# One decoder layer in fp32: the two gates of the mixer as paired Strassen products

## Chip, core and metric

The kernel runs on one core of a Trainium2 chip. The metric is the device time of one execution in microseconds (us). Three executions of the kernel before took 2221.05, 2221.36 and 2223.29 us; their median is 2221.36. TensorE (PE) multiplies, VectorE (DVE) and ScalarE (ACT) do elementwise work, SyncE (SP) issues the transfers (DMAs). Each engine works through its own instructions in a fixed order and waits on semaphores of the others.

## What is computed

```python
D_MODEL = 2048; SEQ = 256; D_FF = 5504; CONV_WIDTH = 1024
x  = LN0(alpha*x + 0.5*SwiGLU_1(x))
z  = x @ W_in        # columns: conv B | C | h | hgrn q | f | i | g | gate_conv (2048) | gate_hgrn (2048)
yA = B * causal_dwconv3(C * h)                   # 256 x 1024
yB = HGRN2(q, f, i, g)                           # 256 x 1024
m  = sigmoid(gate_conv)*(yA @ Wa) + sigmoid(gate_hgrn)*(yB @ Wb)   # the merge
x  = LN1(alpha*x + m @ W_out)
x  = LN2(alpha*x + 0.5*SwiGLU_2(x))
x  = LN3(alpha*x + sigmoid(x @ W_pg) * (p @ W_pp))
```

Everything is float32. The change touches the line of `m`: the two gate products (256 x 2048 by 2048 x 2048 each) and the turning of `m` for the product with `W_out`.

## The kernel before

**Tiles.** The 256 rows are two row tiles t = 0, 1 of 128. The 2048 columns of an operand are 16 k-tiles of 128; products are made in column chunks of 512 (`CC`). A stationary operand (x, ya, yb, m) is kept transposed, 128 x 128 per k-tile, and split into a high and a low part (names ending in h and l), since each fp32 product is done in three reduced-precision passes: wh·xh, wl·xh, wh·xl (L1052 to L1054 before, L1096 to L1098 after). A matmul has 512 columns.

**Weights.** Each element of the plan of weights is 256 rows by 512 columns, 512 KB. SP loads it into a slot `raw`, of which there are four (`NRAW`). ScalarE casts it to `wh` (L985 before, L1029 after), VectorE forms `wl` = raw − wh (L996, L1040); then the raw slot is free for the next load. Six pairs of wh and wl (`NMAIN`) exist; a pair is free when its last matmul is done. `feed()` hands out loads, additions, casts and splits in the order of the plan as slots allow. A scheduler then fixes the order on each engine.

**Units.** A `Unit` is a plain product: for each chunk of columns, blocks of k-tiles are run for both row tiles into two accumulators (PSUM banks; eight exist, handed to roles such as `a` for accumulators and `t` for transposes), and an epilogue works on each. A `Quad` computes two column chunks at once, for both row tiles. The feed-forward stages use it already. Of its 16 k-tiles eight go through Strassen products (Winograd's form): seven products p1 to p7 in place of eight, for which sums of weight elements (`11`, `t1`, `22`, `t3`, `t2`, `21`, `t4` in two steps `.0` and `.1`) are made by VectorE in place (L964 before, L1008 after), and sums of x (s1 to s4) are stationary operands. The other eight k-tiles are plain: elements `a0` to `a3` for the first chunk (into p2 and p4), `u0` to `u3` for the second. The order of its elements is written out in a string. Weights that enter sums have slots of their own (`raw11` two, `raw12`, `raw21`, `raw22` one each: `HIGH`), which exist only in some stages ("regions").

**The merge before.** For each of four chunks c: a Unit x1 · gate_conv of 16 k-tiles with a sigmoid in its epilogue, then a Unit ya · Wa of 8 k-tiles, whose epilogue multiplies; then the same for four chunks of gate_hgrn and yb · Wb, whose epilogue also adds. Finished tiles of m are turned in the background (`defer` puts a step some ticks, that is some elements, later): the six tiles of c < 3 by VectorE in blocks of 32 x 32 (`turn_blocks`, L297), the two of c = 3 by TensorE against an identity (`to_stat`, L274 before, L278 after). Ahead of the merge stands the convolution, whose last steps (`b`, `z`, `gh`/`gl`: the operand ya) run beside the first gate matmuls. The product with W_out follows.

Of the kernel before, what the change touches and what calls it, by code (L numbers as in the profile page):

```python
# [66 lines left out]
class Quad:  # L67
# [18 lines left out]
    ORDER = ("h1 u0 h2 h3 a0 h4 11.0 u1 t1.0 22.0 t3.0 a1 t2.0 21.0 t4.0 "  # L86
             "11.1 u2 t1.1 22.1 t3.1 a2 t2.1 21.1 t4.1").split()
    ORDER8 = ("u3 a3 11.0 u0 t1.0 a0 22.0 t3.0 u1 t2.0 21.0 a1 t4.0 "
              "11.1 u2 t1.1 22.1 t3.1 a2 t2.1 21.1 t4.1").split()

    def __init__(self, stat, w, cols, width, after, short):
        self.stat, self.w, self.cols, self.width, self.after = stat, w, cols, width, after
        self.shorted = not short
        order = self.ORDER if short else self.ORDER8
# [42 lines left out]
def hybrid_layer(ctx: ExitStack, tc: tile.TileContext, x, p, ln_g, ln_b, ffn1_w_in, ffn1_w_out, mix_w_in,  # L137
# [24 lines left out]
    def open_region(kind):  # L162


        if kind.startswith("tail"):
            region.pop("hctx").close()
        region["pool"] = reopen("ctx", kind, "left")
        region["kind"] = kind
        if kind.startswith("lead"):
            region["high"] = reopen("hctx", kind + "h", "right")  # L170
            held.update(dict.fromkeys(HIGH, 0), on=False)
        if kind.startswith("ffn"):
            roles = {"a": 7, "t": 1}
        else:
            roles = {"t": 2, "a": 4, "h": 2}
# [100 lines left out]

    def halves(stat, t, g, src, nb, tag):

        where, bufs = {"m": (region["pool"], 4), "s": (region["pool"], 7)}.get(tag, (op, 8))
# [5 lines left out]
        nc.vector.tensor_tensor(out=lf, in0=src, in1=hf.bitcast(F32), op=ALU.subtract)  # L285
        stat.parts[t, g] = (h, l)

    def to_stat(stat, t, g, src, nb, tag):
        tp = transposed(src, nb)
        halves(stat, t, g, tp[:, : nb * P], nb, tag)  # L290

    def turn_blocks(dst, src, nb):

        cols = src[:, : nb * P].rearrange("p (a b c) -> p a b c", b=4, c=32)
        for q in range(4):
            for b in range(4):
                nc.vector.transpose(dst[32 * b : 32 * b + 32, :nb, 32 * q : 32 * q + 32], cols[32 * q : 32 * q + 32, :, b, :])  # L297

    def to_stat_blocks(stat, t, g, src, nb, tag):
        y = rtile([P, 4, P], F32, tag="hT", name="hT", bufs=2)  # L300
        turn_blocks(y, src, nb)
        halves(stat, t, g, y[:, :nb, :].rearrange("p a b -> p (a b)"), nb, tag)


    plain = {}
# [5 lines left out]
    def plain_tile(t, c):  # L311
# [2 lines left out]
            plain[t, c // 2] = high(("11", "12", "21", "22")[2 * t + c // 2], "yT")  # L314
        return plain[t, c // 2][:, c % 2, :]

    def sums(stat):
        def both(o, a, b, op):
            nc.vector.tensor_tensor(out=o, in0=a, in1=b, op=op)

        def four(x11, x12, x21, x22, s1, s2, s3, s4):
            both(s3, x11, x21, ALU.subtract)
            both(s1, x21, x22, ALU.subtract)
            both(s2, s1, x11, ALU.subtract)
            both(s4, x12, s2, ALU.add)
# [125 lines left out]
    def ffn(name, xs, w_in, w_out, ln_i, nxt):  # L451
# [7 lines left out]
        def in_units(ch, g, ci):  # L459
            c0 = starts[ch]  # L460
            w = starts[ch + 1] - c0
            if ch > 1:
# [33 lines left out]
                def fifth(ps):  # L496
# [8 lines left out]
                units.append(Quad(xs, w_in, (c0, DFF + c0), CC, after, ch < 10))  # L505
                return
            silu = {}

# [286 lines left out]
    conv_units(1)  # L795

    ms = Stat()
    mc = {}

    def gate_units(c, first):  # L800
        sig = {}

        def epi_s(t, acc):
            sig[t] = st.tile([P, CC], F32, tag="silu", name="sig", bufs=2)
            nc.scalar.activation(sig[t], acc, AF.Sigmoid)

        def epi_y(t, acc):
            if first:
                mc[t, c] = rtile([P, CC], tag=f"m{t}{c}", name="m")
                nc.vector.tensor_tensor(out=mc[t, c], in0=sig[t], in1=acc, op=ALU.mult)  # L810
            else:
                m = mc[t, c]
                nc.vector.tensor_tensor(out=sig[t], in0=sig[t], in1=acc, op=ALU.mult)
                nc.vector.tensor_tensor(out=m, in0=m, in1=sig[t], op=ALU.add)
                turn = to_stat_blocks if c < 3 else to_stat
                defer(2, lambda: turn(ms, t, c, m, 4, "g" if c < 2 else "m"))

        base = 7 * CW if first else 7 * CW + D
        units.append(Unit(x1, wm, 0, 16, base + c * CC, CC, epi_s))
        units.append(Unit(ya if first else yb, (branch_w_conv if first else branch_w_hgrn)[0], 0, 8, c * CC, CC, epi_y))  # L820

    units.append(("merge", drain))
    for c in range(4):
# [53 lines left out]
    for u in units:  # L877
# [3 lines left out]
        if isinstance(u, Quad):  # L881
            base = len(plan)
            for el in u.els:
                if "add" in el:
                    adds.append(len(plan))
                    el["behind"] += base
                for key, ks, n in el.get("load", ()):
# [4 lines left out]
                    loads[ring].append((key, kind, u.w, ks[0] * P, len(ks), u.cols[n], u.width))  # L892
# [181 lines left out]
    def run_quad(u, gi):  # L1074
# [5 lines left out]
        for el in u.els:  # L1080
            for i, (bank, t, ks) in enumerate(el["use"]):
                tick()
                first = bank not in ps
                if first:
                    ps[bank] = ptile("a", bank)
# [10 lines left out]
    for u in units:  # L1096
# [2 lines left out]
        elif isinstance(u, Quad):  # L1099
            gi = run_quad(u, gi)  # L1100
        else:
            if u[0] == "merge":
                u[1]()
            if region["kind"] != u[0]:
                open_region(u[0])
            if u[0] != "merge":
                u[1]()
            feed()
    drain()
# [29 lines left out]
```

## Time and profile before

| | |
|---|---|
| runs, median | 2221.36 us |
| profiled execution | 2221.55 us, span 2219.8 us, granted clock 0.996 |
| TensorE busy | 2193.6 us (99%) in 10062 matmuls |
| VectorE busy | 1748.4 us (79%) |
| ScalarE busy | 1142.0 us (51%) |
| DMA | 430 MB, 194 GB/s on average |
| the merge | 1057 us to 1317 us of the span |

A row of the timeline has the start and the length in us, the engine, the line, the operation, what it writes and reads, its shape, and how many alike follow each other (x2); in brackets stands the idle time ahead of it and what ended that. A row of a group has the busy time, the mean length of one in ns, and the idle time ahead. A row of windows has, for a stretch, the busy time of each engine with its number of instructions, the granted clock of TensorE (1.00 is full), the DMA engines' busy share and GB/s. A row on transfers ends with the size of each and the median time from issue to landing in us.

### The profile page before, as it was taken

What the parts mean: (1) busy time and instruction counts of PE and PEld (TensorE: products, weight loads), DVE (VectorE), ACT (ScalarE), POOL (GpSimd) and SP (SyncE); (2) the same over time, 40 slices, a digit from 0 to 9 for tenths busy, and PEclk for the clock granted to TensorE, in tenths of its full rate; (3) what the DMA queues carried; (4) which work ended last, traced back from release to release, by engine and by line L of the source; (5) the groups of instructions that cost most, each with busy time, mean ns of one, the idle gap of its engine ahead of it and who ended that gap; (6) DMA issues with size and microseconds to landing.
All of it is one profiled execution on the core that took longest, in us unless ns stands there. A gap on an engine that the chain in (4) does not pass through costs nothing.

```text
span 2219.8 us, 27083 instructions
## 1 busy us (share of the span) xinstructions
PE 2193.6 (99%) x10062; PEld 1826.8 (82%) x10062; DVE 1748.4 (79%) x2042; ACT 1142.0 (51%) x1357; POOL 10.0 (0%) x32
## 2 busy tenths in 40 slices
PE   9999999999999999999999999999999999999997
PEld 7988888888877888888888888798888888888886
DVE  6799998999885678557555876779999989998668
ACT  5555555555555534434444443645556555555463
POOL 1000000000000000000000000000000000000000
PEclk9999999999999999999999999999999999999999
DMA  7666666666663665554555675566666666665564
GB/s 252 217 191 210 204 205 193 189 200 209 209 199 105 200 197 173 175 167 152 190 190 190 198 228 194 182 200 199 186 199 194 205 213 200 201 209 181 167 224 154
DMA packets 225848, 430.00 MB, mean 194 GB/s; under 512 B 14252, under 2 KB 22964, under 8 KB 225716
## 3 DMA queue, kind: packets, MB, share of 16 engines
q1 hardware_dynamic: 225716, 428.27, 60.9%
q8 instruction: 79, 1.29, 0.2%
q14 instruction: 53, 0.43, 0.1%
HBM read 426.12 MB, written 2.10 MB: 193 GB/s over the span
## 4 chain that ended last, share of the span: by engine, by line
PE 94%; DVE 3%; ACT 1%; DMA 1%; issue 1%; SPq 0%; DVEq 0%; ACTq 0%
PE bank L1052 30%; PE bank L1053 30%; PE bank L1054 30%; PE bank L274 2%; DVE wl L996 1%; PE bank L643 1%; ACT wh L985 1%; DMA raw<-in_ffn_w_out_dram 1%; DMA raw<-in_ffn_w_in_dram 0%; DVE x L444 0%; DVE silu L469 0%; DMA x<-in_x_dram 0%; DVE x L445 0%; ACT y L424 0%; DVE raw L964 0%
## 5 line engine op out<-in xcount | busy, mean ns | idle before, releaser
L985 ACT CAST wh<-raw 128x1024 fp32r<-128x1024 f32 (+2 forms) x944 | 947.8, 1031 | 808.7 <-PE bank L1054 424.2
L996 DVE TENSOR_TENSOR wl<-raw,wh 128x1024 fp32r<-128x1024 f32 (+2 forms) x944 | 1109.7, 1199 | 303.5 <-ACT wh L985 285.3
L1054 PE MATMUL bank<-wh,xl 128*128 128x512 f32 (+1 forms) x1688 | 651.9, 387 | 1.5 <-DVE xl L285 1.5
L1053 PE MATMUL bank<-wl,xh 128*128 128x512 f32 (+1 forms) x1688 | 652.5, 387 | 0.0
L1052 PE MATMUL bank<-wh,xh 128*128 128x512 f32 (+1 forms) x1688 | 644.3, 388 | 1.6 <-ACT xh L284 1.6
L1054 PEld LDWEIGHTS bank<-wh,xl 128*128 128x128 f32 x1688 | 317.8, 188 | 63.2 <-DVE xl L285 2.2
L1052 PEld LDWEIGHTS bank<-wh,xh 128*128 128x128 f32 x1688 | 318.1, 188 | 62.4 <-ACT xh L284 2.3
L1053 PEld LDWEIGHTS bank<-wl,xh 128*128 128x128 f32 x1688 | 318.1, 188 | 60.4 <-DVE wl L996 0.5
L1052 PE MATMUL bank<-wh,gh 128*128 128x512 f32 x896 | 346.7, 392 | 2.8 <-ACT wh L985 1.4
L1053 PE MATMUL bank<-wl,gh 128*128 128x512 f32 x896 | 348.8, 390 | 0.5 <-DVE wl L996 0.3
L1054 PE MATMUL bank<-wh,gl 128*128 128x512 f32 x896 | 348.2, 390 | 0.0
L964 DVE TENSOR_TENSOR raw<-raw,raw 128x1024 f32<-128x1024 f32 (+1 forms) x176 | 206.3, 1172 | 9.2 <-DMA raw<-in_ffn_w_in_dram 8.0
L1052 PEld LDWEIGHTS bank<-wh,gh 128*128 128x128 f32 x896 | 168.1, 188 | 39.5 <-ACT wh L985 4.8
L1053 PEld LDWEIGHTS bank<-wl,gh 128*128 128x128 f32 x896 | 168.3, 188 | 36.4 <-DVE wl L996 2.2
L1054 PEld LDWEIGHTS bank<-wh,gl 128*128 128x128 f32 x896 | 168.2, 188 | 34.8
L1053 PE MATMUL bank<-wl,sh 128*128 128x512 f32 x464 | 181.6, 391 | 0.0
L1054 PE MATMUL bank<-wh,sl 128*128 128x512 f32 x464 | 180.5, 389 | 0.0
L1052 PE MATMUL bank<-wh,sh 128*128 128x512 f32 x464 | 177.1, 389 | 0.0
L1052 PEld LDWEIGHTS bank<-wh,sh 128*128 128x128 f32 x464 | 87.1, 188 | 18.3
L1054 PEld LDWEIGHTS bank<-wh,sl 128*128 128x128 f32 x464 | 87.1, 188 | 17.9
L1053 PEld LDWEIGHTS bank<-wl,sh 128*128 128x128 f32 x464 | 87.1, 188 | 17.8
L284 ACT CAST gh<-bank 128x512 fp32r<-128x512 f32 (+2 forms) x50 | 28.3, 568 | 76.8 <-PE bank L274 75.7
(173 smaller groups left out, 1018.7 us busy)
## 6 DMA issues: line engine op xcount, KB each, us to landing
raw<-in_ffn_w_in_dram SPq DMA_DIRECT2D x288, 512.0 KB, 4.3
raw<-in_mix_w_in_dram SPq DMA_DIRECT2D x176, 512.0 KB, 4.7
raw<-in_ffn_w_out_dram SPq DMA_DIRECT2D x168, 512.0 KB, 4.6
raw<-in_ffn_w_in_dram SPq DMA_DIRECT2D x64, 256.0 KB, 3.0
raw<-in_mix_w_out_dram SPq DMA_DIRECT2D x32, 512.0 KB, 5.1
raw<-in_ple_w_gate_dram SPq DMA_DIRECT2D x32, 512.0 KB, 5.2
raw<-in_ffn_w_in_dram SPq DMA_DIRECT2D x32, 384.0 KB, 3.8
raw<-in_branch_w_conv_dram SPq DMA_DIRECT2D x16, 512.0 KB, 4.5
```

The costliest lines, as they stand in the source:

```text
L274: state["turned"] = nc.tensor.transpose(tp[:, i * P : (i + 1) * P], src[:, i * P : (i + 1) * P], ident).ins
L284: nc.scalar.copy(hf, src)
L643: nc.tensor.matmul(gp[:, (h * 2 + t) * 64 : (h * 2 + t + 1) * 64], kd[:, h, t * P : (t + 1) * P], qd[:, h, t, :], start=True, stop=True)
L964: nc.vector.tensor_tensor(out=out, in0=a, in1=b, op=ALU.add)
L985: nc.scalar.copy(h[:, :n, :w], raw[:, :n, :w])
L996: state["split"] = nc.vector.tensor_tensor(out=l[:, :n, :w], in0=raw[:, :n, :w], in1=h[:, :n, :w].bitcast(F32), op=ALU.subtract).ins
L1052: nc.tensor.matmul(acc, sh, wh[:, a, :n], start=first, stop=False)
L1053: nc.tensor.matmul(acc, sh, wl[:, a, :n], start=False, stop=False)
L1054: nc.tensor.matmul(acc, sl, wh[:, a, :n], start=False, stop=last)
```

## The change

For each c, the chunk of gate_conv and the chunk of gate_hgrn with the same columns become one Quad, with eight k-tiles by Strassen products. Two new orders are added; that of the first quad ("gate0") has all plain elements of the first chunk ahead. Behind each Quad come the Units ya · Wa and yb · Wb of that c. The sums s1 to s4 of x1 are made once, as the merge begins (`gate_sums`): VectorE adds high and low part to get x back, forms the sums, and both engines split them. The plain elements of the second chunk are added into p3 (t = 0) and into p1's bank under the name `r` (t = 1). The merged tiles are kept, and TensorE turns all eight beside the last branch units. The merge gets the regions' high slots and other shares of banks.

```diff
+        "gate": "a0 a1 11.0 11.1 u0 t1.0 a2 22.0 t3.0 u1 t2.0 21.0 a3 t4.0 u2 t1.1 22.1 t3.1 u3 t2.1 21.1 t4.1",
+        "gate0": "a0 a1 a2 a3 11.0 11.1 u0 t1.0 22.0 t3.0 u1 t2.0 21.0 t4.0 u2 t1.1 22.1 t3.1 u3 t2.1 21.1 t4.1",
...
+        second = (("p3", 0), ("r", 1)) if form.startswith("gate") else (("p3", "d"), ("p5", 1))
...
-            made[f"u{i}"] = dict(load=[(None, ks, 1)], use=[("p3", "d", ks), ("p5", 1, ks)])
+            made[f"u{i}"] = dict(load=[(None, ks, 1)], use=[(*to, ks) for to in second])
...
-    def turn_blocks(dst, src, nb):
...
+    def gate_sums():
+        x = []
+        for t in range(NT):
+            for g in range(2):
+                h, l = x1.parts[t, g]
+                x.append(rtile([P, CC], tag=f"m{t}{g}", name="xT"))
+                nc.vector.tensor_tensor(out=x[-1], in0=h.rearrange("p a b -> p (a b)").bitcast(F32),
+                                        in1=l.rearrange("p a b -> p (a b)").bitcast(F32), op=ALU.add)
+        four(*x, x[2], x[0], s3 := rtile([P, CC], tag="m02", name="xT"), x[1])
+        for n, src in (("s1", x[2]), ("s4", x[1]), ("s3", s3), ("s2", x[0])):
+            halves(x1, n, 0, src, 4, "s")
+
+    def gate_units(c):
...
+        def first(ps):
+            made["conv", 0] = work("h")
+            nc.scalar.copy(made["conv", 0], ps["p1"])
+
+        def second(ps):
+            h = made["hgrn", 0] = work("silu")
+            nc.scalar.copy(h, ps["p3"])
+            both(h, h, ps["p5"], ALU.add)
...
+        def fifth(ps):
+            both(made["conv", 1], made["conv", 1], ps["p4"], ALU.add)
+            for key in (("conv", 1), ("hgrn", 0), ("hgrn", 1)):
+                sigmoid(made[key])
+            if c == 3:
+                share_banks({"a": 4, "t": 4})
+                for i in range(4):
+                    defer(1 + 3 * i, lambda t=i % 2, cc=i // 2: to_stat(ms, t, cc, mc[t, cc], 4, "x"))
...
+        cols = (7 * CW + c * CC, 7 * CW + D + c * CC)
+        units.append(Quad(x1, wm, cols, CC, after, "gate" if c else "gate0"))
+        units.append(Unit(ya, branch_w_conv[0], 0, 8, c * CC, CC, epi_c))
+        units.append(Unit(yb, branch_w_hgrn[0], 0, 8, c * CC, CC, epi_h))
...
-    for c in range(4):
-        gate_units(c, True)
-    for c in range(4):
-        gate_units(c, False)
+    for c in range(4):
+        gate_units(c)
```

VectorE as the merge begins, before. z is the last product of the convolution (its second row tile is z_8526), gl the low part of the operand ya; wl are splits of weights.

```order
L783 TENSOR_TENSOR z_8490<-bank2_81,cT_8185 128x512
L996 TENSOR_TENSOR wl_8503<-raw_8384,wh_8502 128x1024
L996 TENSOR_TENSOR wl_8515<-raw_8404,wh_8514 128x1024
L285 TENSOR_TENSOR gl_8493<-z_8490,gh_8492 128x512
L783 TENSOR_TENSOR z_8526<-bank6_85,cT_8185 128x512
L996 TENSOR_TENSOR wl_8567<-raw_8472,wh_8566 128x1024
L285 TENSOR_TENSOR gl_8529<-z_8526,gh_8528 128x512
L996 TENSOR_TENSOR wl_8579<-raw_8484,wh_8578 128x1024
```

Behind z there was one split per element, 256 rows of weights for twelve matmuls. The same place after, a little behind the second z (now z_8514), whose x1 sums xT stand between splits and additions of weights:

```order
L1040 TENSOR_TENSOR wl_8538<-raw11_8527,wh_8537 128x1024
L312 TENSOR_TENSOR xT_8550<-xT_8550,xT_8552 128x512
L1040 TENSOR_TENSOR wl_8541<-raw11_8529,wh_8540 128x1024
L1008 TENSOR_TENSOR raw11_8527<-raw11_8527,raw12_8531 128x1024
L312 TENSOR_TENSOR xT_8546<-xT_8550,xT_8546 128x512
L1040 TENSOR_TENSOR wl_8588<-raw_8384,wh_8587 128x1024
L289 TENSOR_TENSOR sl_8560<-xT_8550,sh_8559 128x512
L1008 TENSOR_TENSOR raw12_8531<-raw12_8531,raw22_8533 128x1024
L312 TENSOR_TENSOR xT_8548<-xT_8548,xT_8546 128x512
L1040 TENSOR_TENSOR wl_8606<-raw11_8527,wh_8605 128x1024
```

From wl_8538 on, a split serves six matmuls where it belongs to a Strassen product; wl_8588 is u0, wl_8606 t1.0, and wl_8697, twelve rows further on, t4.0.

ScalarE at the end of the first quad, after. sig_8852 is the copy of p3 (bank 0); raw_8591 to raw_8767 are the four elements of ya's weights, raw_8820 the first of yb's.

```order
L1029 CAST wh_8791<-raw21_8688 128x1024
L821 COPY sig_8852<-bank0_79 128x512
L1029 CAST wh_8804<-raw11_8529 128x1024
L1029 CAST wh_8816<-raw_8591 128x1024
L1029 CAST wh_8828<-raw_8657 128x1024
L1029 CAST wh_8846<-raw_8713 128x1024
L1029 CAST wh_8861<-raw_8767 128x1024
L1029 CAST wh_8880<-raw_8820 128x1024
```

The copy now stands ahead of the casts of the branch weights; no such copy was in the merge before. TensorE at the same place, after: the last matmuls of t4.1 (wh_8804, bank 3 is p4) and what follows.

```order
L1096 MATMUL bank3_82<-wh_8804,xh_5862 128x512
L1097 MATMUL bank3_82<-wl_8805,xh_5862 128x512
L1098 MATMUL bank3_82<-wh_8804,xl_5863 128x512
L1096 MATMUL bank0_79<-wh_8880,gh_7132 128x512
L1097 MATMUL bank0_79<-wl_8881,gh_7132 128x512
L1098 MATMUL bank0_79<-wh_8880,gl_7133 128x512
L1096 MATMUL bank0_79<-wh_8880,gh_7132 128x512
L1097 MATMUL bank0_79<-wl_8881,gh_7132 128x512
L1098 MATMUL bank0_79<-wh_8880,gl_7133 128x512
L1096 MATMUL bank0_79<-wh_8894,gh_7132 128x512
L1096 MATMUL bank7_86<-wh_8816,gh_7174 128x512
```

The first yb weights (wh_8880, raw_8820, which takes the raw slot of raw_8591) come ahead of those of ya (wh_8816). Over the whole program TensorE has 48 matmuls of 512 columns less and 24 transposes more; VectorE has 96 block transposes less, and 24 splits, 32 weight additions and 44 operations of 512 columns more; the transfers are as many, in another order.

More of the change, by code (lines that the diff above doesn't have):

```diff
@@ L85, with __init__ @@
     PLAIN = ((10, 11), (12, 13), (14, 15), (8, 9))
[L86 to L91, printed above, removed]
+    ORDER = {
[4 rows of a table added]
+    }
+    def __init__(self, stat, w, cols, width, after, form):
         self.stat, self.w, self.cols, self.width, self.after = stat, w, cols, width, after
+        short = form == "short"
         self.shorted = not short
-        order = self.ORDER if short else self.ORDER8
+        order = self.ORDER[form].split()
+        second = (("p3", 0), ("r", 1)) if form.startswith("gate") else (("p3", "d"), ("p5", 1))
         made = {}
@@ L277, in halves @@
     def halves(stat, t, g, src, nb, tag):
-        where, bufs = {"m": (region["pool"], 4), "s": (region["pool"], 7)}.get(tag, (op, 8))
+        where, bufs = (region["pool"], 4 if region["kind"] == "merge" else 7) if tag == "s" else (op, 8)
         h = where.tile([P, 4, P], F32R, tag=tag + "h", name=tag + "h", bufs=bufs)
@@ L290, in to_stat @@
         halves(stat, t, g, tp[:, : nb * P], nb, tag)
-    def turn_blocks(dst, src, nb):
[L294 to L302, printed above, removed]
     plain = {}
@@ L315, in plain_tile, with four @@
         return plain[t, c // 2][:, c % 2, :]
+    def four(x11, x12, x21, x22, s1, s2, s3, s4):
+        for o, a, b, op in ((s3, x11, x21, ALU.subtract), (s1, x21, x22, ALU.subtract),
+                            (s2, s1, x11, ALU.subtract), (s4, x12, s2, ALU.add)):
+            nc.vector.tensor_tensor(out=o, in0=a, in1=b, op=op)
     def sums(stat):
@@ L319, in both @@
             nc.vector.tensor_tensor(out=o, in0=a, in1=b, op=op)
[L321 to L325, printed above, removed]
         lo, hi, spare = [plain[t, 0] for t in range(NT)], [plain[t, 1] for t in range(NT)], high("11", "s")
@@ L504, in in_units @@
                                (("p2",), fourth), (("p4",), fifth)])
-                units.append(Quad(xs, w_in, (c0, DFF + c0), CC, after, ch < 10))
+                units.append(Quad(xs, w_in, (c0, DFF + c0), CC, after, "short" if ch < 10 else "long"))
                 return
@@ L797, in hybrid_layer @@
     ms = Stat()
-    mc = {}
[L800 to L820, printed above, removed]
+    def gate_sums():
[9 more added lines that the diff above has]
+            halves(x1, n, 0, src, 4, "s")
@@ new lines, in gate_units, with both, work, sigmoid @@
+    def gate_units(c):
+        made = {}
+        def both(o, a, b, op):
+            nc.vector.tensor_tensor(out=o, in0=a, in1=b, op=op)
+        def work(tag):
+            return st.tile([P, CC], F32, tag=tag, name="sig", bufs=2 if tag == "silu" else 3)
+        def sigmoid(a):
+            nc.scalar.activation(a, a, AF.Sigmoid)
+        def first(ps):
[5 more added lines that the diff above has]
+            both(h, h, ps["p5"], ALU.add)
+        def third(ps):
+            e = made["conv", 1] = work("silu")
+            h = made["hgrn", 1] = work("h")
+            with tc.issue_after(state["split"]):
+                both(e, made["conv", 0], ps["p6"], ALU.add)
+            both(made["hgrn", 0], made["hgrn", 0], e, ALU.subtract)
+            both(e, e, ps["p7"], ALU.add)
+            both(h, ps["p5"], e, ALU.subtract)
+            both(h, h, ps["r"], ALU.add)
+        def fourth(ps):
+            both(made["conv", 0], made["conv", 0], ps["p2"], ALU.add)
+            sigmoid(made["conv", 0])
+        def fifth(ps):
[6 more added lines that the diff above has]
+                    defer(1 + 3 * i, lambda t=i % 2, cc=i // 2: to_stat(ms, t, cc, mc[t, cc], 4, "x"))
+        def epi_c(t, acc):
+            both(made["conv", t], made["conv", t], acc, ALU.mult)
+            if c == 3:
+                defer(2 + 3 * t, lambda: to_stat(ms, t, 2, mc[t, 2], 4, "g"))
+        def epi_h(t, acc):
+            m = mc[t, c] = made["conv", t] if c == 3 else rtile([P, CC], tag=f"m{t}{c}", name="m")
+            both(made["hgrn", t], made["hgrn", t], acc, ALU.mult)
+            both(m, made["conv", t], made["hgrn", t], ALU.add)
+            if c == 3:
+                defer(2, lambda: to_stat(ms, t, 3, m, 4, "g"))
+        after = deque([(("p1",), first), (("p3", "p5"), second), (("p6", "p7"), third),
+                       (("p2",), fourth), (("p4",), fifth)])
+        cols = (7 * CW + c * CC, 7 * CW + D + c * CC)
+        units.append(Quad(x1, wm, cols, CC, after, "gate" if c else "gate0"))
+        units.append(Unit(ya, branch_w_conv[0], 0, 8, c * CC, CC, epi_c))
+        units.append(Unit(yb, branch_w_hgrn[0], 0, 8, c * CC, CC, epi_h))
@@ L822, in hybrid_layer @@
+    mc = {}
     units.append(("merge", drain))
+    units.append(("merge", gate_sums))
     for c in range(4):
-        gate_units(c, True)
-    for c in range(4):
-        gate_units(c, False)
+        gate_units(c)
     for c in range(4):
@@ L886, in hybrid_layer @@
                     el["behind"] += base
-                for key, ks, n in el.get("load", ()):
+                for key, ks, slab in el.get("load", ()):
                     ring = key[2] if key else "raw"
@@ L1084, in run_quad @@
                 if first:
-                    ps[bank] = ptile("a", bank)
+                    ps[bank] = ps["p1"] if bank == "r" else ptile("a", bank)
                 for a, k in enumerate(ks):
@@ L1101, in hybrid_layer @@
         else:
-            if u[0] == "merge":
-                u[1]()
+            if u[1] is drain:
+                drain()
             if region["kind"] != u[0]:
                 open_region(u[0])
-            if u[0] != "merge":
+            if u[1] is not drain:
                 u[1]()
```

12 lines of the change are left out of this document (5 added, 7 removed), and 2 rows, old and new, of the table ORDER.

## The prediction

> **What bounds the kernel now.** I read the page first (busy shares, chain), then the windows of the stage that changes and of a stage that already works in the way the change will, then the timelines of each engine around the place where the merge begins.
>
> ```profile
> span 2219.8 us, 27083 instructions
> PE 2193.6 (99%) x10062; PEld 1826.8 (82%) x10062; DVE 1748.4 (79%) x2042; ACT 1142.0 (51%) x1357; POOL 10.0 (0%) x32
> PE 94%; DVE 3%; ACT 1%; DMA 1%; issue 1%; SPq 0%; DVEq 0%; ACTq 0%
> ...
> core 0: us, PE busy (x) PEld busy (x) DVE busy (x) ACT busy (x) POOL busy (x), PEclk, DMA share, GB/s
> 200.00:400.00 200.00, 199.65 (x893) 164.60 (x892) 183.57 (x189) 111.65 (x124) 0.00 (x0) 1.00 0.66 205
> 1057.00:1317.00 260.00, 260.00 (x1151) 215.29 (x1150) 162.77 (x223) 114.78 (x121) 0.00 (x0) 1.00 0.60 195
> ```
>
> TensorE carries the whole kernel: 94% of the chain. The last row is the merge, some 260 us: TensorE without a gap, VectorE at 163 of 260 (63%), ScalarE at 44%. So in this stage a matmul less is time won, and work on the other engines is free as long as it arrives in time. The row above it is a stretch of the feed-forward quads, which are Strassen products already: VectorE at 92%, and TensorE still has no gap to speak of. That is the best evidence for the change; but it is a steady state, with a store of prepared weights ahead of TensorE. The question is what happens where the merge enters and leaves such a quad.
>
> **What is removed and added on TensorE.** A pair of column chunks took 16 k-tiles for two row tiles, in three passes, for each of two gates: 2·16·2·3 = 192 matmuls. Half of that by seven products in place of eight makes 180. Over four pairs 48 matmuls of 512 columns go. Six merged tiles that VectorE turned are now turned by TensorE: 24 transposes come.
>
> ```profile
> 1149.81 0.39 PE L1054 MATMUL bank<-wh,gl 128*128 128x512 f32 x1
> ...
> 1179.96 0.39 PE L1052 MATMUL bank<-wh,gh 128*128 128x512 f32 x1
> ...
> 1062.99 0.39 PE L1054 MATMUL bank<-wh,xl 128*128 128x512 f32 x1
> 1063.22 0.60 PE L274 MATMUL bank<-ident,b 128*128 128x128 f32 x4
> 1063.57 0.47 PE L1052 MATMUL bank<-wh,xh 128*128 128x512 f32 x1
> 1063.88 0.39 PE L1053 MATMUL bank<-wl,xh 128*128 128x512 f32 x1
> ```
>
> The first two rows lie 133 matmuls apart: 30.15/133 = 0.2267 us each (0.39 is the length of one; they overlap). So 48 × 0.2267 = 10.9 us go. The other four rows price transposes: between 1062.99 and 1063.88 lie two pitches (0.45) and four transposes, 0.89 in all, so 0.44 for four; 24 cost 2.6 us. Net −8.2 us, if nothing waits.
>
> **What is added elsewhere.** VectorE loses 96 block transposes and gets 32 additions of weights, 24 more splits, 32 elementwise operations of the quads and 12 that form the sums of x1.
>
> ```profile
> L996 DVE TENSOR_TENSOR wl<-raw,wh 128x1024 fp32r<-128x1024 f32 x888 | 1064.4, 1222 | 279.4 <-ACT wh L985 262.0
> L297 DVE STREAM_TRANSPOSE hT<-m 32x128 f32<-32x128 f32 x96 | 29.1, 303 | 1.4
> ...
> 1043.53 2.35 DVE L996 TENSOR_TENSOR wl<-raw,wh 128x1024 fp32r<-128x1024 f32 x2
> 1045.80 0.68 DVE L285 TENSOR_TENSOR gl<-bank,gh 128x512 fp32r<-128x512 f32 x1
> ...
> 1055.87 0.68 DVE L285 TENSOR_TENSOR gl<-bank,gh 128x512 fp32r<-128x512 f32 x1
> 1056.47 0.68 DVE L783 TENSOR_TENSOR z<-bank,cT 128x512 f32<-128x512 f32 x1
> 1057.07 2.53 DVE L996 TENSOR_TENSOR wl<-raw,wh 128x1024 fp32r<-128x1024 f32 x2
> ```
>
> Two wide splits from 1043.53 to the next operation at 1045.80: 1.14 us each back to back (1.22 alone). Narrow ones follow each other by 0.60. Removing the 29.1 us of block transposes pays nothing: TensorE never waited for them. Adding (24+32) × 1.14 + 44 × 0.60 = 90 us to 163 over 250 us makes, less the 29, 224 of 250: 90%, on average below the 92% of the feed-forward window. So the steady part of the quads is costed at nothing, and what covers it is the store of weights (four raw slots, six pairs of wh and wl). The cover is missing at the borders, one by one:
>
> *Start of the first quad.* Here VectorE turns from a stage where it is idle half the time into a queue in fixed order.
>
> ```profile
> 1057.09 0.39 PE L1052 MATMUL bank<-wh,xh 128*128 128x512 f32 x1
> ...
> 1063.85 0.69 DVE L783 TENSOR_TENSOR z<-bank,cT 128x512 f32<-128x512 f32 x1 [3.65 <-PE bank L274]
> ```
>
> 1057.09 is the first gate matmul. The second z waits for transposes that stand 22 matmuls behind it in the changed order: 1057.09 + 22 × 0.227 + 0.6 = 1062.7, and VectorE is free again at 1063.3. The sums of x1 are queued behind this z, and from there to the split of the first t4 (wl_8697) the order has 16 wide and 13 narrow operations: 16 × 1.14 + 13 × 0.60 = 26.0, so it is done at 1089.4. TensorE has 48 matmuls of plain tiles, four transposes, and 69 matmuls of products ahead of the one that needs it: 1057.09 + 117 × 0.2267 + 0.44 = 1084.1. It loses 5.4 us, in several small waits (u0, t1.0, u1, t2.0, t4.0). Bounds: 3.5 if operations overlap by 0.15 in place of the 0.08 read here (29 × 0.07 = 2.0 less), 8 if they do not overlap (16 × 1.22 + 13 × 0.68 = 28.4). I take 5.5, since pitches were read in the same stretch.
>
> The Trainium skill ("VectorE: DVE Perf Modes", section "The DRAIN you can't avoid") says that the next VectorE operation does not start until the pipe is empty; by that rule the loss would be the 8 of the upper end and the total about 2231. The rows above, 1.14 between starts against 1.22 of length, do not bear it out here.
>
> *End of the first quad.* TensorE's order has the first branch weights of yb (wh_8880) right behind the last product. They use the raw slot of ya's first weights, which is free only after these are cast and split; and ScalarE casts them behind a copy that waits for the last matmul into p3.
>
> ```profile
> 1050.50 0.39 PE L1054 MATMUL bank<-wh,xl 128*128 128x512 f32 x1
> ...
> 1050.93 0.59 ACT L777 COPY b<-bank 128x512 f32<-128x512 f32 x1 [4.13 <-PE bank L1054]
> 1052.29 1.05 ACT L985 CAST wh<-raw 128x1024 fp32r<-128x1024 f32 x1 [0.77 <-PE bank L1054]
> ...
> 1053.37 2.59 DVE L996 TENSOR_TENSOR wl<-raw,wh 128x1024 fp32r<-128x1024 f32 x2 [3.63 <-ACT wh L985]
> ...
> 262.46 2.93 ACT L985 CAST wh<-raw 128x1024 fp32r<-128x1024 f32 x3
> ...
> raw<-in_ffn_w_in_dram SPq DMA_DIRECT2D x288, 512.0 KB, 4.3
> raw<-in_mix_w_in_dram SPq DMA_DIRECT2D x176, 512.0 KB, 4.7
> ...
> raw<-in_ple_w_gate_dram SPq DMA_DIRECT2D x32, 512.0 KB, 5.2
> ...
> raw<-in_branch_w_hgrn_dram SPq DMA_DIRECT2D x16, 512.0 KB, 4.6
> ```
>
> From the start of the last p3 matmul: 0.43 until a copy of its bank can start (1050.50 to 1050.93), copy 0.52 (0.59 less the overlap), two casts 0.94 + 1.05 (three took 2.93, the last in full), the split of ya's first weights, which queues shortly behind the one before it, 1.4, then the transfer 4.6, cast 1.05, split 1.14: 11.1 us until the first matmul that needs wl_8881. Between the two stand 23 matmuls, 5.2 us. Loss 5.9 us. Other 512 KB transfers have medians from 4.3 to 5.2, which makes 5.6 to 6.5; a single one may lie further off, so the bounds are 4 and 7.
>
> *Borders of the second and third quad.* There yb's first cast waits for a slot pair that a matmul only seven ahead of its user releases: 0.43 + 1.05 for cast, then VectorE's queue, 3.2 us against 1.8 of matmuls: about 1.5 each, 3.0 for two; 0 if the splits ahead run early, 4 if a transfer is late. The last pair begins ya first, in a bank that is free: 0.
>
> *The clock.* A gap of some 5 us at the end of the first quad may cost once more.
>
> ```profile
> 1413.35 0.68 PE L1054 MATMUL bank<-wh,xl 128*128 128x512 f32 x1 [0.80 <-DVE xl L285]
> 1413.83 0.63 PE L1052 MATMUL bank<-wh,xh 128*128 128x512 f32 x1
> ...
> 1416.38 0.63 PE L1052 MATMUL bank<-wh,xh 128*128 128x512 f32 x1
> 1416.81 0.45 PE L1053 MATMUL bank<-wl,xh 128*128 128x512 f32 x1
> 1417.10 0.40 PE L1054 MATMUL bank<-wh,xl 128*128 128x512 f32 x1
> 1410.00:1440.00 30.00, 28.04 (x124) 22.71 (x125) 25.62 (x40) 24.81 (x47) 0.00 (x0) 0.94 0.62 201
> ```
>
> Behind the layer norm, where TensorE pauses, eight matmuls run at 0.43 instead of 0.23 (granted clock 0.94 over the window): 1.6 us. I count half, 0.8. The Trainium skill ("TensorE: Matmul & The Clock Gate", section "What's actually happening") has the clock halved after an idle window of about 3.4 us; by that rule the gap would cost the full 1.6 when it covers a whole window, and the sum would be 0.8 higher. The rows agree in the factor of two; how long a gap must be, they do not show.
>
> *Edits with one answer.* The copies of p1 and p3 (8 × 0.6) and the four casts of sums are ScalarE work at 51% load and lie beside matmuls, save the p3 copy above. The transfers are as many as before, on the same queue in another order; the high rings are loaded early except three that wait for z, 1063.4, and land by 4.7 us plus queueing, before VectorE reaches them, by the count of operations above at 1069.8 to 1073.3. A later pair, raw12_8642, lands by the same count at about the moment it is needed (1083.3 against 1083.7): part of the upper end. The turning of all tiles at the end has four banks and lies among the last branch units.
>
> **Sum.** −10.9 + 2.6 + 5.5 + 5.9 + 3.0 + 0.8 = +6.9. The profiled execution took 2221.55 us, 0.2 above the median of 2221.36, so 2228.5 for it and 2228.3 as a median; I give 2228.4. A difference under 0.2% (4.4 us: 2216.9 to 2225.8) is what measurement can't tell from none.
>
> **Rivals.**
> 1. *The store covers the borders* (the other side). For it: the feed-forward quads run at 92% VectorE load with 199.65 of 200 us of TensorE, and enter from other stages too. Against it: there the weights of the next unit are in place before it starts; here VectorE gets 16 + 13 operations only after z. Nothing lost gives 2221.4 − 8.2 = 2213.2. It decides when all waits together stay under 3.8 us, for instance if VectorE has the splits done before 1084.
> 2. *Only part of the waits shows.* If the first start costs 5.5 and the second transfer is early, 2221.4 − 8.2 + 5.5 = 2218.7; with both waits of the first quad, but no border after it and no clock loss, 2224.6. All of this is within 0.2%.
> 3. *VectorE becomes the bound in every quad.* If the load of 90% is uneven and each of the later three loses 1 to 3 us more, 2231.5 to 2237. For it: the window of the feed-forward quads leaves only 8% of VectorE. Against it: TensorE had no gaps there.
> 4. That the change doesn't do what it says is excluded: the instruction lists have 48 matmuls less and 24 transposes more.
>
> **How the numbers follow.** Forecast (2225.8 to 2231.5): 0.48. Rival 3 and full clock loss (above 2231.5): 0.14. Rival 2 (2216.9 to 2225.8): 0.28. Rival 1: 0.10. So slower 0.62, same 0.28, faster 0.10. The range 2218 to 2234 leaves out the first rival, the lowest edge of the second and the upper half of the third: two in ten. Cases of both signs hold chance, but the forecast's own range, 2225.8 to 2231.5, follows from the bounds of its terms taken together without all at one end.
>
> **What would show it.** In the profile after: idle time of TensorE ahead of matmuls of wl (L1097) put down to VectorE's split (L1040) in several pieces between 1070 and 1092; one gap of about 5 us near 1104 to 1110, ahead of a matmul with wh and gh (L1096) put down to ScalarE's cast (L1029), with a transfer of branch_w_hgrn just landed; matmuls at 0.43 behind it if the clock falls; one or two gaps over 1 us at each of the next two borders; 24 more transposes at L278 and the block transposes gone. The merge, the 260 us of the window above, should take 267. I am wrong if the first quad is without gaps, which means that VectorE's operations there are shorter or start earlier than 1063.3; if the cast of wh_8880 is ready in time, which means that the slot is freed by another way; or if the gaps are as said but later borders lose more than they are costed at.

## Result and the profile after

Four runs of the changed kernel took 2232.11 to 2234.32 us, median 2233.93, against 2221.78 for the kernel before on the same chip: the ratio is 1.0052, 95% interval 1.0035 to 1.0070. The change makes the kernel 12 us slower, in the direction forecast, 0.07 us inside the upper end of the range (2218 to 2234) and 5.5 above the point of 2228.4.

The profiled execution has a span of 2232.3 us, 12.5 more than before. First the page of the profile after:

```profile
PE 2192.5 (98%) x10038; PEld 1823.3 (82%) x10038; DVE 1809.8 (81%) x2046; ACT 1173.6 (53%) x1393; POOL 10.1 (0%) x32
...
PE 90%; DVE 4%; DMA 2%; ACT 2%; issue 1%; SPq 0%; DVEq 0%; ACTq 0%
```

TensorE's share of the chain falls from 94% to 90%; VectorE, transfers and ScalarE take what it loses. TensorE's waits, grouped by line and by what ended them (total us, times, longest), say at whom it waits. Only the last two rows come from the kernel before:

```profile
PE bank L1096 <- ACT wh L1029: 10.6, 7, 5.7
PE bank L1097 <- DVE wl L1040: 2.9, 5, 0.8
...
PE bank L1052 <- ACT wh L985: 1.4, 1, 1.4
PE bank L1053 <- DVE wl L996: 0.3, 2, 0.2
```

Before, TensorE waited 1.4 us for ScalarE's casts and 0.3 for VectorE's splits; now it waits 10.6 for casts and 2.9 for splits. Where these waits stand is told by the timeline of TensorE after, the start of the first quad and then the ends of the first three:

```profile
1071.71 0.50 PE L1096 MATMUL bank<-wh,sh 128*128 128x512 f32 x1 [0.69 <-ACT wh L1029]
...
1075.78 0.50 PE L1097 MATMUL bank<-wl,sh 128*128 128x512 f32 x1 [0.70 <-DVE wl L1040]
...
1080.32 0.50 PE L1096 MATMUL bank<-wh,sh 128*128 128x512 f32 x1 [1.77 <-ACT wh L1029]
...
1087.82 0.50 PE L1096 MATMUL bank<-wh,xh 128*128 128x512 f32 x1 [0.18 <-ACT wh L1029]
1088.77 0.74 PE L1096 MATMUL bank<-wh,xh 128*128 128x512 f32 x2 [0.44 <-ACT wh L1029]
1089.35 0.40 PE L1097 MATMUL bank<-wl,xh 128*128 128x512 f32 x1
...
1103.45 0.39 PE L1098 MATMUL bank<-wh,xl 128*128 128x512 f32 x1
1109.54 0.80 PE L1096 MATMUL bank<-wh,gh 128*128 128x512 f32 x1 [5.70 <-ACT wh L1029]
1110.80 0.80 PE L1097 MATMUL bank<-wl,gh 128*128 128x512 f32 x1 [0.46 <-DVE wl L1040]
...
1115.66 0.58 PE L1098 MATMUL bank<-wh,gl 128*128 128x512 f32 x1
1116.08 0.39 PE L1096 MATMUL bank<-wh,gh 128*128 128x512 f32 x1
...
1176.59 0.50 PE L1096 MATMUL bank<-wh,gh 128*128 128x512 f32 x1 [0.72 <-ACT wh L1029]
1177.85 0.50 PE L1097 MATMUL bank<-wl,gh 128*128 128x512 f32 x1 [0.76 <-DVE wl L1040]
...
1241.51 0.50 PE L1096 MATMUL bank<-wh,gh 128*128 128x512 f32 x1 [1.05 <-ACT wh L1029]
1242.77 0.50 PE L1097 MATMUL bank<-wl,gh 128*128 128x512 f32 x1 [0.76 <-DVE wl L1040]
```

The places are the ones forecast: several waits between 1070 and 1090, one gap of 5.7 us ahead of yb's first weights, matmuls 0.43 apart behind it until 1116.08, and a pair of gaps, 0.7 to 1.1 us each, at the next two borders. The fourth quad, behind which the banks are shared out anew, has none. In one point the pattern differs. At the start the waits were forecast ahead of matmuls of wl and put down to VectorE's splits; four of the five stand ahead of matmuls of wh and are put down to ScalarE's casts. The casts in turn wait for VectorE, which adds the weights that they cast, as before the wait at 1080.32:

```profile
1079.22 2.00 ACT L1029 CAST wh<-raw 128x1024 fp32r<-128x1024 f32 x2 [1.64 <-DVE raw L1008]
```

So VectorE's queue is the bound there, as forecast, mostly through its additions and not through its splits. From the second z at 1062.20 to 1089 VectorE's rows have no idle time.

To add this up, the best measure is the interval from the first gate matmul to the first matmul behind the layer norm that follows the merge, within one trace. It is 354.72 us before (1057.09 to 1411.81) and 366.36 after (1056.57 to 1422.93): +11.64. (The merge alone was forecast to take 267 us in place of 260; with the product with W_out counted as unchanged, the interval makes it 272.) The rest of the 12.5 lies outside it: −0.5 ahead of the merge, and +1.4 behind the norm. All of that last part is there within 13 us: the changed kernel is 1.1 us late at the fifteenth matmul behind the norm's first one and 1.5 at the fortieth; later stretches give and take some tenths. The 1.1 come nearly all from the clock: TensorE's matmuls run 0.43 apart for longer. In the kernel before they did so up to 1416.81, 5.0 us behind the first; after the change, with waits of nearly the same lengths ahead, up to 1429.88, 7.0 us behind:

```profile
1429.45 0.63 PE L1097 MATMUL bank<-wl,xh 128*128 128x512 f32 x1
1429.88 0.49 PE L1098 MATMUL bank<-wh,xl 128*128 128x512 f32 x1
```

The granted clock is 0.89 in the 30 us from 1421, where it was 0.94 in the 30 us from 1410.

### The profile page after: what moved, and what is told of

It reads as the page before. It is cut to its first block, busy times and chain, and to the rows that moved or that the text cites. A ratio compares the mean times of both kernels' runs of the same rounds, so it can differ in the third digit from the quotient of the medians.

```text
span 2232.3 us, 27072 instructions
## 1 busy us (share of the span) xinstructions
PE 2192.5 (98%) x10038; PEld 1823.3 (82%) x10038; DVE 1809.8 (81%) x2046; ACT 1173.6 (53%) x1393; POOL 10.1 (0%) x32
## 4 chain that ended last, share of the span: by engine, by line
PE 90%; DVE 4%; DMA 2%; ACT 2%; issue 1%; SPq 0%; DVEq 0%; ACTq 0%
PE bank L1097 29%; PE bank L1096 29%; PE bank L1098 29%; DVE wl L1040 2%; PE bank L278 2%; ACT wh L1029 1%; PE bank L634 1%; DVE raw L1008 1%; DMA raw<-in_branch_w_hgrn_dram 1%; DMA raw<-in_ffn_w_in_dram 0%; DMA raw<-in_ffn_w_out_dram 0%; DVE silu L460 0%; DVE x L435 0%; DMA raw<-in_mix_w_in_dram 0%; DMA x<-in_x_dram 0%
## 5 line engine op out<-in xcount | busy, mean ns | idle before, releaser
L1029 ACT CAST wh<-raw 128x1024 fp32r<-128x1024 f32 (+1 forms) x968 | 971.9, 1031 | 802.3 <-PE bank L1098 409.8
L1040 DVE TENSOR_TENSOR wl<-raw,wh 128x1024 fp32r<-128x1024 f32 (+1 forms) x968 | 1137.1, 1201 | 266.7 <-ACT wh L1029 249.4
L1008 DVE TENSOR_TENSOR raw<-raw,raw 128x1024 f32<-128x1024 f32 x208 | 245.0, 1181 | 10.6 <-DMA raw<-in_ffn_w_in_dram 7.4
L1097 PE MATMUL bank<-wl,sh 128*128 128x512 f32 x528 | 206.9, 392 | 0.7 <-DVE wl L1040 0.7
L1098 PE MATMUL bank<-wh,sl 128*128 128x512 f32 x528 | 205.7, 390 | 0.0
L1096 PE MATMUL bank<-wh,sh 128*128 128x512 f32 x528 | 202.4, 390 | 2.5 <-ACT wh L1029 2.5
L1096 PEld LDWEIGHTS bank<-wh,sh 128*128 128x128 f32 x528 | 99.1, 188 | 23.8 <-ACT wh L1029 3.2
L1097 PEld LDWEIGHTS bank<-wl,sh 128*128 128x128 f32 x528 | 99.2, 188 | 21.7 <-DVE wl L1040 1.5
L1098 PEld LDWEIGHTS bank<-wh,sl 128*128 128x128 f32 x528 | 99.2, 188 | 20.2
```

The source lines that it names most:

```text
L1008: nc.vector.tensor_tensor(out=out, in0=a, in1=b, op=ALU.add)
L1029: nc.scalar.copy(h[:, :n, :w], raw[:, :n, :w])
L1040: state["split"] = nc.vector.tensor_tensor(out=l[:, :n, :w], in0=raw[:, :n, :w], in1=h[:, :n, :w].bitcast(F32), op=ALU.subtract).ins
L1096: nc.tensor.matmul(acc, sh, wh[:, a, :n], start=first, stop=False)
L1097: nc.tensor.matmul(acc, sh, wl[:, a, :n], start=False, stop=False)
L1098: nc.tensor.matmul(acc, sl, wh[:, a, :n], start=False, stop=last)
```

## The experiments

**The banks at the ends of the quads.** A Unit takes the accumulator banks that were *first written* longest ago. In both new orders the plain elements a0 and a1 come first, so p2 and p4 are opened first, and they are read out last. ya's two accumulators got these very banks, so that it could not start; yb's had those of p1 and p3, and p3 is read early, and so TensorE's order had yb's weights first, whose transfer starts last. The first run gives the banks out in the order in which they are read:

```diff
             gi += 1
+        if "r" in ps:
+            for name in ("p3", "p6", "p7", "p5", "p1", "p2", "p4"):
+                n = next(n for n in banks if banks[n] is ps[name])
+                used_at[n] = max(used_at.values()) + 1
         return gi
```

> The branch products are given the accumulator banks in the order in which the quad's results are read out (p3, p6, p7, p5, p1, p2, p4) in place of the order in which they were first written; nothing else is changed. Theory A (the gaps at the ends of the quads come from ya's first accumulator standing in p2's bank, which is read last, so that TensorE's order has yb's weights first, whose raw slot and transfer come late): TensorE starts ya at once; the 6.9 us at the end of the first quad, the 2.6 us of matmuls at half clock behind it and the 4.1 us at the ends of the second and third quad go, 13.6 us in all: about 2220.3. Theory B (the raw slots and the transfer set the gap whoever is first, because VectorE splits the branch weights late): ya's own first split ends at about 1103, so a gap of some us stays, and yb's weights are late 11 us later too: 2226 to 2231. Theory C (the gaps come from the copy of p3 that ScalarE has ahead of the casts): no change, 2234.

2219.79 us (10 runs), level with the kernel before on that chip, 2220.81 (ratio 0.9996, 0.9987 to 1.0005). The changed kernel was 12.2 above its kernel before, this one is 1.0 below: 13.2 us are won, and the interval falls by 13.6, from 366.36 to 352.81. Theory A. TensorE at the end of the first quad in this run (its wh,gh is now ya's):

```profile
1101.81 0.39 PE L1096 MATMUL bank<-wh,xh 128*128 128x512 f32 x1
1102.03 0.39 PE L1096 MATMUL bank<-wh,gh 128*128 128x512 f32 x1
1102.26 0.39 PE L1097 MATMUL bank<-wl,xh 128*128 128x512 f32 x1
...
1108.17 1.05 ACT L1029 CAST wh<-raw 128x1024 fp32r<-128x1024 f32 x1 [4.24 <-DMA raw<-in_branch_w_hgrn_dram]
```

No pause is left, at this end or at the later ones: all that TensorE still waits for casts and splits up to the layer norm are three waits at the start of the first quad (0.7, 0.7 and 1.8 us). The ScalarE row shows that yb's first weights land as late as in the changed kernel (cast at 1108.17, there at 1108.45); what changed is that 48 matmuls of ya now lie in front of them. So theory B falls, and theory C with it: the copy of p3 still stands ahead of the casts. The windows from 1102 to 1245 of the two kernels, first the run, then the changed kernel:

```profile
1102.00:1175.00 73.00, 73.00 (x323) 60.44 (x322) 65.33 (x67) 43.32 (x48) 0.00 (x0) 1.00 0.70 223
1175.00:1245.00 70.00, 70.00 (x310) 57.97 (x309) 57.60 (x57) 37.36 (x39) 0.00 (x0) 1.00 0.64 202
...
1102.00:1175.00 73.00, 66.83 (x282) 54.45 (x281) 57.67 (x56) 38.47 (x40) 0.00 (x0) 0.93 0.60 195
1175.00:1245.00 70.00, 66.71 (x291) 54.16 (x290) 58.16 (x59) 38.26 (x40) 0.00 (x0) 1.00 0.62 199
```

TensorE is busy without a break with VectorE at 89% and 82%: the quads are not bound by VectorE in their steady part.

At the start of the first quad this run has the same three first waits as the changed kernel, but a different clock behind the third of them:

```profile
1079.45 0.50 PE L1096 MATMUL bank<-wh,sh 128*128 128x512 f32 x1 [1.77 <-ACT wh L1029]
...
1080.38 0.63 PE L1096 MATMUL bank<-wh,xh 128*128 128x512 f32 x1
...
1083.37 0.46 PE L1096 MATMUL bank<-wh,xh 128*128 128x512 f32 x1
```

From 1080.38 to 1083.37 seven pitches are 0.43; the changed kernel had 0.23 behind its wait of 1.77 us at 1080.32, at a granted clock of 1.00. So the length of one pause alone does not say whether the clock falls.

**VectorE's queue at the start.** The next run forms no sums of x1:

```diff
-        four(*x, x[2], x[0], s3 := rtile([P, CC], tag="m02", name="xT"), x[1])
-        for n, src in (("s1", x[2]), ("s4", x[1]), ("s3", s3), ("s2", x[0])):
-            halves(x1, n, 0, src, 4, "s")
+        for i, n in enumerate(("s1", "s2", "s3", "s4")):
+            x1.parts[n, 0] = x1.parts[i % 2, i // 2]
```

> Leaves out the forming of the sums of x1 (8 additions and 4 splits of 512 columns on VectorE, 4 casts on ScalarE, as the merge begins); parts of x1 stand in their place, so every matmul is still done, on other numbers. Theory A (VectorE's queue behind z makes the waits at the start of the first quad, 5.8 us): 12 x 0.60 = 7.2 us less in the queue takes 4 to 5.8 us away: 2228 to 2230. Theory B (the waits are those for the transfers into the high slots, of which three are issued only behind z): less than 2 us goes: 2232 to 2234.

2227.78 us (7 runs), 7.0 above the kernel before on that chip where the changed kernel was 12.2 above: 5.2 less, as theory A has it. The interval falls by 6.2, from 366.36 to 360.19, a little more than its upper end. TensorE from 1057 to 1090, this run and then the changed kernel:

```profile
1057.00:1090.00 33.00, 33.00 (x150) 27.31 (x149) 27.80 (x26) 17.67 (x20) 0.00 (x0) 1.00 0.67 219
...
1057.00:1090.00 33.00, 29.13 (x123) 22.23 (x122) 28.44 (x32) 16.38 (x21) 0.00 (x0) 1.00 0.53 176
```

No wait is left at the start, so the transfers into the high slots (theory B) were in time. Four casts on ScalarE went with the sums, so this run alone does not tell VectorE's queue from ScalarE's; the run with GpSimd below does, since it leaves the casts where they are.

**The clock.** 22 matmuls that nobody reads are put into the gap:

```diff
+            if "r" in ps and u.cols[0] == 7 * CW and el is u.els[-1]:
+                fill = ptile("t", "fill")
+                for _ in range(22):
+                    nc.tensor.matmul(fill, u.stat.get(1, 4)[0], pairs[gi][0][:, 0, :], start=True, stop=True)
             consumed(gi)
```

> Adds 22 matmuls of 512 columns that nobody reads (into the bank for transposes) at the end of the first quad, 5.0 us of work in a gap of 5.9 us. Theory A (the matmuls behind the gap run at half clock because TensorE paused): they run at 0.23 us, 2.6 us go: about 2231.4. Theory B (they are slow for another reason, for instance because ScalarE and VectorE feed them late one by one): no change, 2234, and the rows behind the gap still stand 0.43 apart.

2232.73 us (4 runs; 2230.68 to 2233.36), too close to tell from medians of two chips, so both kernels ran once more on one chip:

> The changed kernel once more, beside the next run on the same chip: 2233 to 2234 by all theories.

> The 22 matmuls that fill the gap, beside the changed kernel on the same chip. Theory A (half clock behind the gap costs 2.2 us, as the interval between the first gate matmul and the layer norm had it): 2.2 us below the changed kernel. Theory B (nothing is won, as the two medians from different chips against their kernel before had it): within 0.5 us of it.

2232.90 us for the changed kernel (2231.01 to 2234.63) and 2231.60 with the fill (2230.09 to 2234.03). The medians differ by 1.3 where single runs spread over 3.6, which by itself decides nothing. The traces do: the interval is 366.36 and 366.48 in the two of the changed kernel, 364.14 and 363.68 in the two with the fill, 2.5 less on average. The rows behind the gap, in the first run with the fill:

```profile
1111.31 0.50 PE L1097 MATMUL bank<-wl,gh 128*128 128x512 f32 x1 [0.76 <-DVE wl L1040]
1111.64 0.40 PE L1098 MATMUL bank<-wh,gl 128*128 128x512 f32 x1
1111.88 0.39 PE L1096 MATMUL bank<-wh,gh 128*128 128x512 f32 x1
1112.11 0.40 PE L1097 MATMUL bank<-wl,gh 128*128 128x512 f32 x1
```

The same matmuls, 0.23 apart in place of 0.43, though VectorE's first two splits of yb's weights start no earlier (1110.03 and 1112.97, in the changed kernel 1109.52 and 1111.86). The pause was what made them slow (theory A).

**The sums on GpSimd.** With the banks of the first run, GpSimd forms x1 and its sums:

```diff
-                nc.vector.tensor_tensor(out=x[-1], in0=h...bitcast(F32), in1=l...bitcast(F32), op=ALU.add)
-        four(*x, x[2], x[0], s3 := ..., x[1])
+                nc.gpsimd.tensor_tensor(out=x[-1], in0=h...bitcast(F32), in1=l...bitcast(F32), op=ALU.add)
+        four(nc.gpsimd, *x, x[2], x[0], s3 := ..., x[1])
```

> The banks of the first run, and the 8 additions that form x1 again and its sums are made by GpSimd, which has nothing else to do there, in place of VectorE; the 4 splits of the sums stay on VectorE. Theory A (VectorE's queue behind z): 8 x 0.60 = 4.8 us less in it; if GpSimd takes no more than some 1.2 us for each, the sums come in time and 3 to 4.8 us go on top of the first run: 2215.5 to 2217.5, which is faster than the kernel before. Theory B (GpSimd is too slow, over 2 us each): the first matmul with s1, due at 1074, waits for six additions in a row and the gain turns into a loss of 2 to 6 us: 2222 to 2227.

2218.24 us (10 runs; ratio to the kernel before 0.9988, 0.9979 to 0.9998). The interval falls to 348.75, 4.1 below the first run's 352.81, within theory A: with the casts unchanged, it was VectorE's queue that held the first quad up. But the median fell by 1.6 only. The trace has a new wait ahead of the merge. GpSimd starts as soon as its data are there. The rows of GpSimd, VectorE and TensorE at that time, and last VectorE's row in the first run:

```profile
1021.77 2.54 POOL L797 TENSOR_TENSOR xT<-xh,xl 128x512 f32<-128x512 f32 x2 [47.06 <-DVE qd L648]
1026.31 3.54 POOL L797 TENSOR_TENSOR xT<-xh,xl 128x512 f32<-128x512 f32 x2 [2.00 <-DVE kb L649]
1029.81 6.59 POOL L312 TENSOR_TENSOR xT<-xT 128x512 f32<-128x512 f32 x4
...
1028.61 3.99 DVE L757 TENSOR_SCALAR cT<-uT,cw 128x128 f32<-128x128 f32 x4
...
1037.20 0.66 PE L278 MATMUL bank<-ident,u 128*128 128x128 f32 x4 [1.72 <-DVE u L748]
...
1027.69 0.88 DVE L757 TENSOR_SCALAR cT<-uT,cw 128x128 f32<-128x128 f32 x4
```

The next run holds GpSimd back with a copy of one column of cT:

```diff
+                if j == 1 and t == 1:
+                    state["cT"] = nc.gpsimd.tensor_copy(mark, cT[:, 3, S - 1 : S]).ins
...
+        with tc.issue_after(state["cT"]):
             (the additions and sums of the run before)
```

> As the run before with GpSimd's sums, but GpSimd starts them only when the convolution's cT is done (about 1042 in place of 1021). Theory A (while GpSimd worked at 1021 to 1036, VectorE's operations on cT were locked out, 3.99 us for four in place of 0.88, and TensorE waited 1.7 us for the u behind them; at 1042 VectorE has only operations that can wait): the gap of 1.7 us at 1037 goes, the merge stays as it was: about 2216.5, 0.2% below the kernel before. Theory B (VectorE's splits and z at 1043 to 1060 are locked out as well and come late): the waits move to the first gate matmuls, 2218 to 2221.

2216.27 us (11 runs) against 2220.65 for the kernel before: ratio 0.9982, 95% interval 0.9974 to 0.9991. Theory A: the gap at 1037 is gone, the interval up to the layer norm is 349.16, and this version is faster than both kernels, than the one before by 4.4 us of the 8.2 that the change saves on paper. What is left at the start of its first quad are waits of 1.06, 0.18 and 0.44 us for casts.

**The head start.** Last, the first quad in the order of the others, with the banks of the first run:

```diff
-        units.append(Quad(x1, wm, cols, CC, after, "gate" if c else "gate0"))
+        units.append(Quad(x1, wm, cols, CC, after, "gate"))
```

> The banks of the first run; the first quad takes the order of the other three, with two plain elements ahead of the first product in place of four. Theory A (what counts at the start is the number of operations that VectorE has between z and the split of t4.0, against 117 matmuls): two more wide splits, 2 x 1.14 us, come behind z, so 2.3 us more than the first run, about 2222. Theory B (what counts is the head start of plain matmuls, 24 x 0.227 us less of it): 5.4 us more, about 2225. Theory C (the store evens it out): the same as the first run, 2219.8.

2221.99 us (10 runs), 1.3 above the kernel before on that chip where the first run was 1.0 below; the interval 355.12 against 352.81, 2.3 more. Theory A. The waits moved forward,

```profile
1063.34 0.49 PE L1096 MATMUL bank<-wh,xh 128*128 128x512 f32 x1 [1.92 <-ACT wh L1029]
1066.48 0.80 PE L1097 MATMUL bank<-wl,xh 128*128 128x512 f32 x1 [2.65 <-DVE wl L1040]
```

and of the 4.6 us waited here the interval keeps 2.3: the rest would have been lost later. What counts is how much VectorE has to do between z and t4.0.

## Why the forecast was right, and where it was too small

- **Saved and added on TensorE: −8.2.** It stands to within 0.9. With the run that has both repairs the interval is 354.72 − 349.16 = 5.6 shorter than before, and its rest of waits is 1.7: 7.3 of 8.2. The other 0.9 no wait explains, as with 0.4 in the sum below. Whether a transpose costs more than 0.11 there was not tried.
- **Start of the first quad: 5.5 forecast, 5.8 measured.** The first matmul that needs wl_8697 starts at 1089.35; 1056.57 + 117 × 0.2267 + 0.44 = 1083.53. The count of VectorE's operations behind z held, and so did their pitch: z started at 1062.20, 0.5 earlier than worked out, as the whole merge did.
- **End of the first quad: 5.9 forecast, 6.9 measured** (1110.80 against 1103.45 plus two pitches, 1103.90). The chain was the one described. Its mis-sized term is the transfer:

```profile
1099.31 2.99 SPq L969 DMA_DIRECT2D raw<-in_mix_w_in_dram  x2
1103.07 3.77 SPq L969 DMA_DIRECT2D raw<-in_branch_w_hgrn_dram  x4
...
1108.45 1.04 ACT L1029 CAST wh<-raw 128x1024 fp32r<-128x1024 f32 x1 [4.01 <-DMA raw<-in_branch_w_hgrn_dram]
```

  5.4 us from issue to cast in place of 4.6, 0.8 of the 1.0, with two transfers for the next quad issued just ahead; whether those made it slower was not tried. The copy of p3 and the slot of raw_8591 were steps of the chain, but why TensorE needed yb's weights first at all was not asked: the order of the banks. This was the lever, as the first run showed.
- **Second and third border: 3.0 forecast, 4.2 measured** (1.9 and 2.2), above the bound of 4. Here the step was another one than forecast. The prediction had yb's first cast wait for a slot pair that a matmul releases; the trace has it wait for the transfer of yb's weights, as in the first quad:

```profile
1175.49 1.05 ACT L1029 CAST wh<-raw 128x1024 fp32r<-128x1024 f32 x1 [1.21 <-DMA raw<-in_branch_w_hgrn_dram]
```

  The matmul seven ahead of the user started at 1174.12, so by the forecast's 0.43 the pair was free at 1174.55, 0.9 earlier. The cause behind both is the order of the banks: the first run removed these gaps too. "Later borders lose more than they are costed at" was one of the prediction's own signs of being wrong, and it came true by 1.2 us.
- **Clock: 0.8 forecast, 2.6 measured.** Of all terms this was mis-sized most: it was entered at half of what the layer norm's rows had shown, and the slow stretch was longer, twelve pitches from 1110.80 to 1116.08 in place of eight (5.28 − 12 × 0.2267 = 2.6). The page of the Trainium skill that the prediction weighed ("TensorE: Matmul & The Clock Gate", "What's actually happening") has the clock back after a free-running window of about 3.4 us that is busy throughout, so, as an estimate from that page, 3.4 to 6.8 us after the restart; 6.5 us, from 1109.54 to 1116.08, agree with that. The prediction looked for a loss of clock at this gap alone; the longer slow stretch behind the layer norm, some 1 us of the span, had no term.
- **Sum.** −8.2 + 5.8 + 6.9 + 4.2 + 2.6 = 11.3 (11.2 before rounding) of the 11.6 in the interval; together with −0.5 ahead and +1.4 behind it, the 12.5 of the span.
- **The rivals.** The store does not cover the borders, but not because six pairs and four slots are too few: with banks in the right order the same store covers all ends. VectorE as the bound in every quad is excluded by the windows above.
- **Where it landed.** The prediction gave 0.48 to 2225.8 to 2231.5 and 0.14 to what came, above 2231.5, under the heading of rival 3 and a full loss of clock. Rival 3 did not happen; the clock loss did, and was larger than its full 1.6. Direction and places were right by the working. All four terms of loss came out too small, and that the time still lies inside the range, by 0.07 us, is luck.

## What to carry to other kernels

Saved matmuls are won only if TensorE finds its next operand ready where one stage meets the next; count the in-order queue of the feeding engine from the last thing it must wait for, against the matmuls up to its user. When accumulators are handed out in rotation, rotate by when they are *read out*, not by when they were first written: an order of weights that looks late can be the shadow of a bank that is not free. A pause of TensorE costs its length and can cost slow matmuls behind it: 2.6 us behind the one of 5.7 us here. Short pauses are not safe from this either: the same wait of 1.77 us kept the clock in one run and lost it for seven pitches in another.

## What the hardware showed beside that

While GpSimd added fp32 tiles (1.3 to 1.8 us each), VectorE's short operations were held up far beyond their length: four tensor_scalar of 128 x 128 took 3.99 us in place of 0.88. In the run that delays GpSimd, VectorE at 1046 to 1051, where GpSimd was busy, had these rows:

```profile
1046.08 2.32 DVE L1045 TENSOR_TENSOR wl<-raw,wh 128x1024 fp32r<-128x1024 f32 x1
...
1049.60 1.21 DVE L375 TENSOR_TENSOR u<-u,m 128x4 f32<-128x4 f32 x1
```

A split of 2.32 us in place of 1.22, and 1.21 for four elements per row, which took 0.16 to 0.17 before. TensorE had no wait between 1036 and 1077 in that run, so it cost nothing there. The Trainium skill ("SBUF — State Buffer", "Who interferes with whom") describes a port pair that the two engines share, taken by one instruction at a time in full; an operation on four elements per row that takes 1.21 us, most of the 1.5 us of one GpSimd addition at that time (four in 6.02 us), is what that would give.
